# A transformer layer on one core: where residual rows are scaled, how the last pair's sum is formed, and which queue asks for the first x tile

## The chip, the core and the metric

The kernel runs on one core of a Trainium2 chip. Five engines of the core take part, each with an instruction stream of its own: TensorE (PE; its weight loads are listed as PEld), VectorE (DVE), ScalarE (ACT), GpSimd (POOL) and SyncE (SP). SP does no arithmetic here; it issues transfers, and so do ACT and POOL at some places. An engine works its stream in order: an instruction that waits holds up everything behind it on that engine, and this goes for the transfers in the queues of SP, ACT and POOL too. The 16 DMA engines of the core carry what all queues ask for.

The metric is the device time of one execution in microseconds (us). Times are compared as the median of several executions.

## The reference, cut to what matters

One layer of a streaming encoder over 1024 prompt rows and 8 x 16 = 128 sample rows of width 1024, all in float32:

```python
def trunk_layer(x, ckv_past, kpe_past, conv_past, ...):
    mix, ckv, kpe, v = token_mixer(x, ...)          # latent attention and a spatial-gating branch, then w_o
    h = layer_norm(DEEPNORM_ALPHA * x + mix, ln1_g, ln1_b)
    ff, conv_state = conv_ffn(h, conv_past, w_up, w_conv, b_conv, w_down)
    y = layer_norm(DEEPNORM_ALPHA * h + ff, ln2_g, ln2_b)
    return y, ckv, kpe, v, conv_state

def conv_ffn(x, conv_past, w_up, w_conv, b_conv, w_down):
    up = x @ w_up                                    # 1024 -> 2 * 2816
    padded = concat([conv_past, up])
    conv = b_conv + sum(w_conv[k] * padded[k:k + s_len] for k in range(3))
    a, g = split(conv, 2)
    return (silu(a) * g) @ w_down, padded[-2:]       # 2816 -> 1024
```

For this change the two uses of `h` matter: it is the input of the up projection, and `ALPHA * h` is added again at the end. `h` is a normalised row times `ln1_g` plus `ln1_b`.

## The kernel before, in words

The rows stand in nine tiles of 128 (eight of the prompt, `t` = 0 to 7, and one of samples, `t` = 8 = `NP`). Every float32 product is formed of three matmuls: an operand is split into a rounded part, which ACT copies (L60), and the rest, which DVE subtracts (L61); products are high by high, high by rest, rest by high (L72 to L74, `dmm` from L1211, `product_mm` at L936 to L938).

The stages, with their places in the profiled execution:

- **Latents (from 0).** `w1` (eight pieces `w1[k]` of 128x704) and the tiles of x, transposed (`xT`), are loaded by SP, split, and multiplied. The sample tile comes first (`ORD[0]`), in three pieces of 1, 3 and 4 blocks of 128 columns, and the pieces of `w1` are asked for in between (L183 to L197). ACT's first instruction is the load of a table.
- **Attention, gating branch, output projection, first layer norm (up to about 472 us).** At its end a tile of normalised rows, without `ln1_g` and `ln1_b`, is in `yt`, goes to the scratch tensor `nd[t]` in device memory (L843), and is transposed on PE; there ACT applies `ln1_g` and `ln1_b` for the up projection (L859).
- **Up stage (about 472 to 960 us).** 22 turns `i` of some 22.4 us. A turn has 14 products (seven combinations `STEPS` of sub-blocks for each of two halves of the rows, in the manner of Strassen), whose results ACT copies or DVE adds into the buffers `U` (L1035, L1037). POOL prepares `U` for the next turn (`new_U`, L1014 and L1015). The conv, the silu and the gate of turn `i` (`after(i)`) are a list of small functions `pend`, of which one is called behind each product of turn `i + 1`; the last of them send the results out by POOL (`ad`, `an`, `ax`). `lg1`, the row `ln1_g` spread over the partitions, is loaded at the start of the stage and lies in the last part of `cbox`.
- **Down stage (about 960 to 1218 us).** Five phases "2", "1", "65", "73", "4", each with 11 entries `p`. `produce` makes the next entry's operands: SP loads a weight tile (`raw` or `rw`) and an activation tile (`ra`), DVE forms sums of them ("65": L1133, L1134, L1146; "73": L1140), and ACT and DVE split them into slots of a ring of 14. `fill_ring` calls `produce` until the ring is full, and then the entry's matmuls are issued. The ring and two kinds of raw buffers (three and two) set how far ahead the loads may run.
- **Residual.** `first_y(t)` (L1206) loads `nd[t]` into `y[t]` and multiplies and adds on DVE (L1208, L1209, 128x1024 each). It is called at the entries 1, 3, 5, 7 of "2" and 1, 3, 5, 7, 9 of "1". `lb1`, `ln1_b` spread over the partitions, is loaded at the start of the stage (L1194). `lg2` and `lb2` are loaded at entry 2 of "1" (L1265, L1266).
- **Takes.** At the end of a phase DVE adds the PSUM banks to `y` (`take`, L1222). A bank that the next phase goes on adding to can't be written by PE until its take is done. At the end of "1" these are four takes of `X` and two of the sample tile; at the end of "65" four of `X` and four of `Z`.
- **Second layer norm and the end.** The sample tile is complete after "1". Its norm is done alone (`norm_a`, `norm_b`) at the entries 3 and 5 of "65"; SP sends it out (`out_y_s`, L1253). The even column halves of the last four tiles get their last product, phase "4", at the very end. For the last tile it is done in two quarters of 256 columns, both in the bank `X[3]`; DVE adds `ALPHA * y` and the bank (L1338), takes statistics (L1339) and normalises (L1340 to L1347).

`pin` keeps an instruction at its place in the program order; what isn't pinned may be moved by the scheduler.

Of the kernel before, what the change touches and what calls it, by code (L numbers as in the profile page):

```python
# [16 lines left out]
P = 128  # L17
D = 1024
# [24 lines left out]
def trunk(tc, a, o):  # L43
# [137 lines left out]

    ORD = [NP] + list(range(NP))
    load_w1(0)  # L183
    for t, cuts in ((ORD[0], (0, 1, 4, 8)), (ORD[1], (0, 4, 8))):
        raw = w1p.tile([P, KD, P], F32, tag="xr", name="xr", bufs=2)
        xq[t] = w1p.tile([P, 2, KD, P], F32R, tag="xs", name="xs", bufs=3)
        for k0, k1 in zip(cuts, cuts[1:]):
            ks = slice(k0, k1)
            sp.dma_start(raw[:, ks], a["xT"][t][:, ks])
            if k1 == 1:  # L190
                dve.tensor_copy(xq[t][:, 0, ks], raw[:, ks])
                dve.tensor_tensor(xq[t][:, 1, ks], raw[:, ks], f(xq[t][:, 0, ks]), ALU.subtract)
            else:
                split(xq[t][:, 0, ks], xq[t][:, 1, ks], raw[:, ks])
                load_w1(len(w1))
# [615 lines left out]
    nd = [drp.tile([P, D], F32, tag=f"nd{t}", name=f"nd{t}") for t in range(TT)]  # L811
    HT, NPF = SEQ // 2, NF // 2
    ad = [drp.tile([P, UW - 2], F32, tag=f"ad{i}", name=f"ad{i}") for i in range(NF)]
    an = [drp.tile([P, SEQ], F32, tag=f"an{i}", name=f"an{i}") for i in range(NPF)]
# [172 lines left out]
    for s in (3, 4):  # L987
        build_h(bop2, 1, s)

    cwst = raw_w()  # L990
    cw = cwst[:, :8 * NF].rearrange("p (f k) -> p f k", k=4)
# [159 lines left out]
    for i in range(NF):  # L1151
# [28 lines left out]
        while pend:  # L1180
            pend.pop(0)()
        pend = after(i)
    while pend:
        pend.pop(0)()
    pool.dma_start(o["cs"], cs)
    upool.release()
    stp.release()
# [4 lines left out]
    half = [slice(0, HT), slice(HT, D)]  # L1192
    lb1 = raw_w()
    pin(sp.dma_start(lb1, a["ln1_b"].partition_broadcast(P)))  # L1194
    y = [y2.tile([P, D], F32, tag=f"y{t}", name=f"y{t}") for t in range(4)]
# [10 lines left out]
    def first_y(t):  # L1206
        pin(sp.dma_start(y[t], nd[t]))
        pin(dve.tensor_tensor(y[t], y[t], lg1, ALU.mult))  # L1208
        pin(dve.tensor_tensor(y[t], y[t], lb1, ALU.add))  # L1209

# [49 lines left out]
    for k, (ph, p) in enumerate(ENTRY[:4 * NPF]):  # L1260
        fill_ring(2)
        if (ph, p) in ylate:
            first_y(ylate[ph, p])
        if (ph, p) == ("1", 2):
            pin(sp.dma_start(lg2, a["ln2_g"].partition_broadcast(P)))  # L1265
            pin(sp.dma_start(lb2, a["ln2_b"].partition_broadcast(P)))  # L1266
        if (ph, p) == ("65", 3):
            lone_n = norm_a([NP], [ctile[2][:, :D]])
        if (ph, p) == ("65", 5):
            norm_b(lone_n)  # L1270
# [40 lines left out]
    fin = made[4 * NPF:]  # L1311
    def end_mm(tp, cols):
        for p, (wd, ac, _) in enumerate(fin):
            dmm(X[tp][:, cols], ac, seg[tp], wd, cols, False, False, p == P1)

# [3 lines left out]
    mv = y2.tile([P, 2], F32, tag="mv", name="mv")  # L1319
    quart = [slice(e * 256, (e + 1) * 256) for e in range(4)]  # L1320
    zs = [ctile[2][:, :D]] + [new_a[1]() for _ in range(3)]
    evens = norm_a(range(4), zs)
# [4 lines left out]
    for tp in range(NT - 1):  # L1327
        take(tp + NT, 0, X[tp], True, True)
        cur = norm_a([tp + NT], [zs[tp]])
        if tp < 2:  # L1330
            end_mm(tp + 1, half[0])
        else:
            end_mm(tp + 1, quart[0])
            end_mm(tp + 1, quart[1])
        norm_b(cur)
    for e in (0, 1):
        yv = yt[:, quart[e]]
        pin(dve.scalar_tensor_tensor(yv, yv, ALPHA, X[3][:, quart[e]], ALU.mult, ALU.add))  # L1338
        pin(dve.bn_stats(s6[:, e], yv))  # L1339
# [123 lines left out]
```

## Time and profile before

| | |
|---|---|
| time, median of 3 executions | 1228.17 us (1227.75 to 1228.61) |
| the profiled execution | 1228.54 us |
| its span | 1226.8 us |
| granted TensorE clock, mean | 0.994 |
| busy: PE / DVE / ACT / POOL | 1202.2 / 917.2 / 573.0 / 100.5 us |
| bytes moved | 156.86 MB, mean 128 GB/s |

The span runs from the first to the last instruction of the profiled execution, which took 1.7 us longer than its span. PE is busy for 98% of it, so what any other engine does matters only where PE waits for it. The rows in the prediction are of these kinds. A row of the **timeline** has the start, the duration, the engine, the line and the operation, and in brackets how long the engine stood idle before it and what it waited for. A row of the **waits** has who waited for what: the sum, how often, and the longest. A row of the **windows** has a stretch of time, its length, then the busy time of PE, PEld, DVE, ACT and POOL with the number of instructions, the granted clock (1.00 is full speed), the share of the DMA engines and GB/s.

### The profile page before, as it was taken

To read this page: it belongs to the slowest core of one execution; us is meant where nothing else is said; L and a number is where in the kernel's file an instruction comes from. 1 tells how busy PE (TensorE), PEld (TensorE's weight loads), DVE (VectorE), ACT (ScalarE), POOL (GpSimd) and SP (SyncE) were. 2 spreads that over 40 slices of the span, in tenths; PEclk is the share of its full clock that TensorE was granted. 3 is DMA by queue.
4 is the path that set the end of the run, shared out by engine and by line. 5 is a ranking of instruction groups with operands and counts; after the bars stand their busy time and mean duration, and the time that the engine had idled before them with its cause. 6 is when DMAs were issued, how large, how long until landed. Compare 5 with 4: busy or idle time off the path is not lost.

```text
span 1226.8 us, 19873 instructions
## 1 busy us (share of the span) xinstructions
PE 1202.2 (98%) x7620; PEld 1117.1 (91%) x7620; DVE 917.2 (75%) x1727; ACT 573.0 (47%) x1154; POOL 100.5 (8%) x255
## 2 busy tenths in 40 slices
PE   8999999999999999999999999999999999899997
PEld 7999999989888888999999999999999988687886
DVE  5767878665557677897777778778778789987667
ACT  5434666542134546654544544545445455344431
POOL 0110002300000001121011011011011100010000
PEclk9999999999999999999999999999999999899999
DMA  7201003551023430132132133123224399878623
GB/s 255 84 21 41 33 22 95 180 176 52 1 85 133 150 120 35 58 128 100 53 116 103 50 117 117 52 100 117 72 81 163 112 401 362 320 287 315 191 78 137
DMA packets 56479, 156.86 MB, mean 128 GB/s; under 512 B 7568, under 2 KB 11536, under 8 KB 56384
## 3 DMA queue, kind: packets, MB, share of 16 engines
q1 hardware_dynamic: 47456, 124.03, 29.1%
q0 software_dynamic: 8928, 31.56, 6.8%
q8 instruction: 60, 0.98, 0.3%
q14 instruction: 35, 0.29, 0.1%
HBM read 119.29 MB, written 36.27 MB: 127 GB/s over the span
## 4 chain that ended last, share of the span: by engine, by line
PE 84%; DVE 6%; DMA 5%; ACT 2%; issue 2%; SPq 1%; DVEq 0%; ACTq 0%
PE A L938 8%; PE A L937 8%; PE A L936 8%; PE A L72 5%; PE A L73 5%; PE A L74 5%; PE D L72 4%; PE D L73 4%; PE D L74 4%; PE D L938 4%; PE D L937 4%; PE D L936 4%; DVE b L61 2%; PE B L938 2%; PE B L936 2%; PE B L937 2%
## 5 line engine op out<-in xcount | busy, mean ns | idle before, releaser
L936 PE MATMUL A<-b,wu 128*128 128x288 f32 x704 | 207.6, 296 | 0.5 <-DVE U L1035 0.4
L937 PE MATMUL A<-b,wu 128*128 128x288 f32 x704 | 207.9, 296 | 0.0
L938 PE MATMUL A<-b,wu 128*128 128x288 f32 x704 | 206.2, 298 | 0.0
L936 PEld LDWEIGHTS A<-b,wu 128*128 128x128 f32 x704 | 132.4, 188 | 1.0 <-DVE U L1035 0.6
L937 PEld LDWEIGHTS A<-b,wu 128*128 128x128 f32 x704 | 132.8, 189 | 0.0
L938 PEld LDWEIGHTS A<-b,wu 128*128 128x128 f32 x704 | 131.1, 188 | 0.0
L60 ACT ACTIVATE wu<-sc 128x512 fp32r<-128x512 f32 x66 | 41.8, 633 | 138.0 <-PE A L938 107.4
L938 PE MATMUL D<-b,wu 128*128 128x288 f32 x352 | 104.9, 298 | 0.0
L936 PE MATMUL D<-b,wu 128*128 128x288 f32 x352 | 104.1, 296 | 0.0
L937 PE MATMUL D<-b,wu 128*128 128x288 f32 x352 | 104.0, 295 | 0.0
L60 ACT ACTIVATE b<-ra 128x512 fp32r<-128x512 f32 (+1 forms) x69 | 45.3, 677 | 64.2 <-PE B L1213 18.1
L1043 DVE SCALAR_TENSOR_TENSOR cbox<-U,raw,cbox 128x1168 f32<-128x1168 f32 x44 | 62.9, 1430 | 9.3 <-ACT cbox L1042 9.3
L61 DVE TENSOR_TENSOR wu<-sc,wu 128x512 fp32r<-128x512 f32 x66 | 46.1, 699 | 29.9 <-ACT wu L60 28.4
L61 DVE TENSOR_TENSOR b<-ra,b 128x512 fp32r<-128x512 f32 (+1 forms) x69 | 50.4, 751 | 22.1 <-ACT b L60 16.0
L937 PEld LDWEIGHTS D<-b,wu 128*128 128x128 f32 x352 | 66.4, 189 | 0.0
L936 PEld LDWEIGHTS D<-b,wu 128*128 128x128 f32 x352 | 66.1, 188 | 0.3 <-ACT b L60 0.3
L938 PEld LDWEIGHTS D<-b,wu 128*128 128x128 f32 x352 | 66.1, 188 | 0.0
L1042 ACT ACTIVATE cbox<-U,raw 128x1168 f32<-128x1168 f32 x44 | 60.0, 1364 | 9.9 <-issue 5.2
L60 ACT ACTIVATE wu<-raw 128x512 fp32r<-128x512 f32 x66 | 41.6, 632 | 47.8 <-PE D L938 23.6
L1044 DVE SCALAR_TENSOR_TENSOR cbox<-U,raw,cbox 128x1168 f32<-128x1168 f32 x44 | 62.9, 1430 | 0.8
L1037 ACT ACTIVATE U<-A 128x288 f32<-128x288 f32 (+2 forms) x154 | 53.3, 369 | 20.7 <-PE A L938 20.7
L61 DVE TENSOR_TENSOR wu<-raw,wu 128x512 fp32r<-128x512 f32 x66 | 45.0, 684 | 15.9 <-ACT wu L60 15.8
(447 smaller groups left out, 3460.0 us busy)
## 6 DMA issues: line engine op xcount, KB each, us to landing
raw<-in_w_up SPq DMA_DIRECT2D x44, 512.0 KB, 3.2
raw<-in_w_down SPq DMA_DIRECT2D x28, 512.0 KB, 6.0
ad<-cbox POOLq DMA_DIRECT2D x22, 584.0 KB, 3.1
ra<-ad SPq DMA_DIRECT2D x40, 256.0 KB, 4.5
rw<-in_w_down SPq DMA_DIRECT2D x16, 512.0 KB, 5.9
xr<-in_xT SPq DMA_DIRECT2D x14, 512.0 KB, 4.0
an<-cbox POOLq DMA_DIRECT2D x11, 512.0 KB, 3.9
ra<-an SPq DMA_DIRECT2D x11, 512.0 KB, 6.8
```

What stands on the lines that cost most here:

```text
L60: act.activation(hi, src, AF.Copy)
L61: dve.tensor_tensor(lo, src, f(hi), ALU.subtract)
L72: pe.matmul(out, lh, rh, start=first, stop=False)
L73: pe.matmul(out, lh, rl, start=False, stop=False)
L74: pe.matmul(out, ll, rh, start=False, stop=last)
L936: hold(pe.matmul(o_, lh, rh, start=first and k == 0, stop=False, skip_group_check=not first))
L937: hold(pe.matmul(o_, lh, rl, start=False, stop=False, skip_group_check=not first))
L938: hold(pe.matmul(o_, ll, rh, start=False, stop=k == 3, skip_group_check=not first))
L1037: act.activation(dst, src, AF.Copy)
L1042: act.activation(v, U[:, 2:n + 2], AF.Identity, bias=cw[:, fi, 3:4], scale=cw[:, fi, 2:3])
L1043: dve.scalar_tensor_tensor(v, U[:, 1:n + 1], cw[:, fi, 1:2], v, ALU.mult, ALU.add)
L1044: dve.scalar_tensor_tensor(v, U[:, 0:n], cw[:, fi, 0:1], v, ALU.mult, ALU.add)
```

## The change

Three things are changed.

**The first x tile.** The three pieces of `xT[ORD[0]]` are asked for by ACT, ahead of its table load, and no longer by SP between the pieces of `w1`.

**The residual rows.** `ln1_g` and `ln1_b` are applied in the up stage. `scale_rows(j)`, for `j` = 0 to 17, does one half (512 columns) of one tile: POOL loads the piece of `nd[t]`, DVE multiplies and adds, POOL stores the piece to a new scratch tensor `hd[t]`. The halves of `ln1_b` are loaded by POOL, twice 128x512. One call stands at the third place of `pend` in each of the turns 1 to 18. `first_y` only loads `hd[t]`, and the load of `lb1` is gone. With that, three things of the down stage move: the loads of `lg2` and `lb2` from entry 2 of "1" to entry 1 of "73", and the two parts of the sample tile's norm from the entries 3 and 5 of "65" to 4 and 6 of "73".

**The end.** The two quarters of the last tile's last product go to two banks of their own (`XL`), and `ALPHA * y` plus the bank `X[3]` is formed ahead of it. The adds behind the product are plain ones of 256 columns.

```diff
@@ latents
     ORD = [NP] + list(range(NP))
+    xraw = [w1p.tile([P, KD, P], F32, tag="xr", name="xr", bufs=2) for _ in range(2)]
+    for k0, k1 in ((0, 1), (1, 4), (4, 8)):
+        tc.keep_in_program_order(act.dma_start(xraw[0][:, k0:k1], a["xT"][ORD[0]][:, k0:k1]))
     load_w1(0)
     for t, cuts in ((ORD[0], (0, 1, 4, 8)), (ORD[1], (0, 4, 8))):
-        raw = w1p.tile([P, KD, P], F32, tag="xr", name="xr", bufs=2)
+        raw = xraw[0] if t == ORD[0] else xraw[1]
...
-            sp.dma_start(raw[:, ks], a["xT"][t][:, ks])
+            if t == ORD[1]:
+                sp.dma_start(raw[:, ks], a["xT"][t][:, ks])
@@ up stage
+    hd = [drp.tile([P, D], F32, tag=f"hd{t}", name=f"hd{t}") for t in range(TT)]
...
+    hx = alloc("hx", side="right")
+
+    def scale_rows(j):
+        c, t = divmod(j, TT)
+        cols = slice(c * 512, (c + 1) * 512)
+        lb = hx.tile([P, 512], F32, tag="lb", name="lb") if t == 0 else lbs[0]
+        if t == 0:
+            lbs[:] = [lb]
+            pool.dma_start(lb, a["ln1_b"][cols].partition_broadcast(P))
+        v = hx.tile([P, 512], F32, tag="hv", name="hv")
+        pool.dma_start(v, nd[t][:, cols])
+        dve.tensor_tensor(v, v, lg1[:, cols], ALU.mult)
+        dve.tensor_tensor(v, v, lb, ALU.add)
+        pool.dma_start(hd[t][:, cols], v)
+
+    lbs = []
...
         pend = after(i)
+        if 1 <= i <= 2 * TT:
+            pend.insert(2, lambda i=i: scale_rows(i - 1))
...
+    hx.release()
@@ down stage
-    lb1 = raw_w()
-    pin(sp.dma_start(lb1, a["ln1_b"].partition_broadcast(P)))
...
     def first_y(t):
-        pin(sp.dma_start(y[t], nd[t]))
-        pin(dve.tensor_tensor(y[t], y[t], lg1, ALU.mult))
-        pin(dve.tensor_tensor(y[t], y[t], lb1, ALU.add))
+        pin(sp.dma_start(y[t], hd[t]))
...
-        if (ph, p) == ("1", 2):
+        if (ph, p) == ("73", 1):
             pin(sp.dma_start(lg2, a["ln2_g"].partition_broadcast(P)))
             pin(sp.dma_start(lb2, a["ln2_b"].partition_broadcast(P)))
-        if (ph, p) == ("65", 3):
+        if (ph, p) == ("73", 4):
             lone_n = norm_a([NP], [ctile[2][:, :D]])
-        if (ph, p) == ("65", 5):
+        if (ph, p) == ("73", 6):
             norm_b(lone_n)
@@ end
-    def end_mm(tp, cols):
+    def end_mm(tp, cols, out=None):
         for p, (wd, ac, _) in enumerate(fin):
-            dmm(X[tp][:, cols], ac, seg[tp], wd, cols, False, False, p == P1)
+            if out is None:
+                dmm(X[tp], ac, seg[tp], wd, cols, False, False, p == P1)
+            else:
+                dmm(out, ac, seg[tp], wd, cols, True, p == 0, p == P1)
...
+    XL = [bank("D") for _ in range(2)]
+    pin(dve.scalar_tensor_tensor(yt[:, half[0]], yt[:, half[0]], ALPHA, X[3], ALU.mult, ALU.add))
...
-            end_mm(tp + 1, quart[0])
-            end_mm(tp + 1, quart[1])
+            for e in range(2):
+                end_mm(tp + 1, quart[e], XL[e][:, :256])
...
-        pin(dve.scalar_tensor_tensor(yv, yv, ALPHA, X[3][:, quart[e]], ALU.mult, ALU.add))
+        pin(dve.tensor_tensor(yv, yv, XL[e][:, :256], ALU.add))
```

At the end of phase "1", DVE's stream before was this; the numbered `y0` to `y3` and `cbox` ahead of the arrow in the rows of L1222 are the residual tiles that the six takes add to, `A`, `B`, `C` the PSUM banks, and the rows of L1133, L1134 and L1146 form the operands of entry 4 of "65":

```order
L1208 TENSOR_TENSOR cbox_5515<-cbox_5515 128x1024
L61 TENSOR_TENSOR b17_5498<-ra_11493,b17_5498 128x1024
L1133 TENSOR_TENSOR rw_11529<-rw_11529 128x512
L1209 TENSOR_TENSOR cbox_5515<-cbox_5515,raw_10843 128x1024
L1134 TENSOR_TENSOR rw_11529<-raw_11531,rw_11529 128x512
L1146 TENSOR_TENSOR raw_11531<-raw_11531,rw_11529 128x512
L1222 SCALAR_TENSOR_TENSOR y0_10845,sums_10855<-y0_10845,A_11216 128x512
```

The same place of the same stream with the change, where the lines are numbered 20 or 21 higher:

```order
L61 TENSOR_TENSOR b17_5507<-ra_11580,b17_5507 128x1024
L1154 TENSOR_TENSOR rw_11614<-rw_11614 128x512
L1155 TENSOR_TENSOR rw_11614<-raw_11616,rw_11614 128x512
L1167 TENSOR_TENSOR raw_11616<-raw_11616,rw_11614 128x512
L1242 SCALAR_TENSOR_TENSOR y0_10950,sums_10960<-y0_10950,A_11313 128x512
```

The multiply and the add of the last residual tile (L1208, L1209) are gone from between the operands; the takes stand where they stood, behind the three sums of entry 4 of "65".

At the end of phase "65", SP's stream before had the store of the sample tile, `out_y_s`, between the loads of the last entry of "65" (L1131, L1132) and those of the first entry of "73" (L1136 to L1139):

```order
L1131 DMA raw_11772<-in_w_down 128x1024
L1132 DMA ra_11769<-an10_4485 128x1024
L1253 DMA out_y_s<-cbox_5515 128x1024
L1136 DMA raw_11816<-in_w_down 128x512
L1137 DMA raw_11816<-in_w_down 128x512
```

With the change SP's stream has it far behind, between the loads of the entries 1 and 2 of "4":

```order
L1141 DMA ra_12295<-ad3_4465 128x512
L1142 DMA raw_12296<-td1_4507 128x512
L1273 DMA out_y_s<-cbox_5527 128x1024
L1141 DMA ra_12335<-ad5_4467 128x512
L1142 DMA rw_12336<-td2_4508 128x512
```

The store, and with it the wait for the norm of the sample tile, has moved behind all loads of "73".

At the head, SP's stream before went back and forth between pieces of `w1` (L152) and pieces of the first x tile (`xr_107`, L189):

```order
L152 DMA raw_102<-in_w1 128x704
L189 DMA xr_107<-in_xT 128x128
L189 DMA xr_107<-in_xT 128x384
L152 DMA raw_115<-in_w1 128x704
L189 DMA xr_107<-in_xT 128x512
L152 DMA raw_123<-in_w1 128x704
```

With the change ACT's stream begins with these three pieces (L185), and its splits of `w1[0]` and `w1[1]` (L60) both come ahead of that of the second x piece:

```order
L185 DMA xr_102<-in_xT 128x128
L185 DMA xr_102<-in_xT 128x384
L185 DMA xr_102<-in_xT 128x512
L60 ACT_TABLE_LOAD
L60 ACTIVATE w1_0_109<-raw_107 128x704
L60 ACTIVATE w1_1_119<-raw_117 128x704
L60 ACTIVATE xs_112<-xr_102 128x384
```

SP is left with the pieces of `w1` alone, one behind the other, up to the third.

## The prediction

> **What bounds the kernel now.** First the page, to see which engine sets the end, then the waits of that engine.
>
> ```profile
> span 1226.8 us, 19873 instructions
> ...
> PE 84%; DVE 6%; DMA 5%; ACT 2%; issue 2%; SPq 1%; DVEq 0%; ACTq 0%
> ```
>
> The chain that ended last runs 84% over PE. So time is won only where PE stands idle, where it runs at a lower clock, and behind its last product. Its waits are few:
>
> ```profile
> PE A L72 <- ACT w L60: 5.8, 2, 4.7
> PE A L1212 <- DVE y L1222: 4.8, 2, 2.9
> ...
> PE D L1214 <- DVE b L61: 1.1, 1, 1.1
> ...
> PE A L936 <- DVE U L1035: 0.4, 1, 0.4
> ```
>
> The first row is the head, the second and third are the ends of the phases "1" and "65". The last is all that the up stage's 22 turns make PE wait for DVE's adds into U. Then the windows, which show what a pause costs beside itself, and how full the other engines are:
>
> ```profile
> 545.00:580.00 35.00, 35.00 (x265) 35.00 (x264) 27.11 (x40) 15.44 (x32) 3.94 (x12) 1.00 0.27 97
> 1000.00:1040.00 40.00, 40.00 (x179) 33.11 (x178) 38.35 (x53) 21.99 (x36) 0.00 (x0) 1.00 1.00 365
> 1066.68:1072.84 6.16, 6.16 (x15) 4.83 (x16) 6.16 (x14) 1.34 (x2) 0.29 (x1) 0.54 0.46 161
> 1125.95:1130.60 4.65, 4.65 (x13) 3.66 (x14) 4.65 (x9) 1.21 (x2) 0.00 (x0) 0.63 0.91 346
> 1140.00:1160.00 20.00, 20.00 (x90) 16.57 (x89) 11.57 (x13) 9.90 (x13) 0.00 (x0) 1.00 0.52 162
> ```
>
> In the up stage (first row) PE is full and DVE busy for 27.11 of 35 us. In the down stage (second row) DVE and the DMA engines are both full: 38.35 of 40, and a share of 1.00. There PE runs on a stock of operands that DVE and the loads can only just fill. The next two rows are what follows the two pauses: clock 0.54 and 0.63. At full clock a matmul of these phases takes 40.00 / 179 = 0.223 us (second row). So 15 matmuls should take 3.35 us and took 6.16, 2.81 lost; 13 should take 2.90 and took 4.65, 1.75 lost.
>
> **Residual rows, first place: the end of "1".**
>
> ```profile
> 1063.01 0.73 PE L1214 MATMUL D<-b,b 128*128 128x512 f32 x2 [1.10 <-DVE b L61]
> 1066.68 0.80 PE L1212 MATMUL A<-b,b 128*128 128x512 f32 x1 [2.94 <-DVE y L1222]
> ...
> 1060.60 1.22 DVE L1208 TENSOR_TENSOR cbox<-cbox 128x1024 f32<-128x1024 f32 x1
> 1061.74 1.22 DVE L61 TENSOR_TENSOR b<-ra,b 128x1024 fp32r<-128x1024 f32 x1
> 1063.47 1.22 DVE L1209 TENSOR_TENSOR cbox<-cbox,raw 128x1024 f32<-128x1024 f32 x1
> 1064.61 0.68 DVE L1134 TENSOR_TENSOR rw<-raw,rw 128x512 f32<-128x512 f32 x1
> 1065.94 0.68 DVE L1222 SCALAR_TENSOR_TENSOR y<-y,A 128x512 f32<-128x512 f32 x1
> ...
> 1064.96 1.06 ACT L60 ACTIVATE b<-ra 128x1024 fp32r<-128x1024 f32 x1 [4.59 <-DMA ra<-an]
> ```
>
> PE pauses 1.10 for a split that stood behind L1208, and 2.94 for the first take, which stood behind L1209 and the sums of the next entry. With the lost clock this place costs 1.10 + 2.94 + 2.81 = 6.85 us. The change takes away 9 multiplies and 9 adds of 1.22, so 22 us of DVE's work between 992 and 1065:
>
> ```profile
> L1208 DVE TENSOR_TENSOR y<-y,cbox x7: 1218/1218/1219, 992.3 to 1049.2; 128x1024 f32<-128x1024 f32 x7
> ...
> L908 DVE TENSOR_TENSOR sc<-raw 128x512 f32<-128x512 f32 x17 | 11.6, 684 | 1.5 <-DMA raw<-in_w_up 1.4
> 558.78 0.52 DVE L1035 TENSOR_TENSOR U<-U,A 128x160 f32<-128x160 f32 x2 [1.68 <-PE A L938]
> 565.03 0.10 POOL L1014 MEMSET U<- 128x2 f32 x1 [3.83 <-ACT U L1037]
> td<-raw POOLq DMA_DIRECT2D x3, 256.0 KB, 4.8
> ```
>
> It also takes 1.5 MB of loads out of this stretch (lb1, lg2 and lb2, 0.5 MB each, the last two moved behind it), which at the 365 GB/s of the second window are 4.1 us of full DMA engines. What is late next is the sum of entry 4 of "65", which the takes still stand behind. Its weights had landed by 1064.61 at the latest, where L1134 reads them; its activations (ACT's row, landed near 1064.9) aren't in the sum. Even if that was their landing, with the loads 4.1 earlier L1134 could run at 1060.5, and two sums and a take of 0.69 each let PE go on near 1062.6. Without the pause of 1.10 PE runs out of other work at 1066.68 - 2.94 - 1.10 = 1062.6. So by the loads alone, at their worst, the pause is about nil; by DVE, with 22 us less, it is nil with room. I take the whole 6.85 as gone, with 0.3 left over for a take that is just late. If the loads gain nothing, since they only run further ahead, the 2.94 and its clock stay: a rival below.
>
> **Second place: the end of "65".**
>
> ```profile
> SPq L1131 <- DVE b L61: 31.3, 8, 6.7
> SPq L1253 <- DVE cbox L1252: 11.2, 1, 11.2
> ...
> 1109.57 0.69 DVE L1140 TENSOR_TENSOR raw<-raw 128x512 f32<-128x512 f32 x1 [5.38 <-DMA raw<-in_w_down]
> 1123.99 1.21 DVE L61 TENSOR_TENSOR b<-ra,b 128x1024 fp32r<-128x1024 f32 x1
> 1125.13 0.67 DVE L1222 SCALAR_TENSOR_TENSOR y<-y,A 128x512 f32<-128x512 f32 x1
> 1125.95 0.47 PE L1212 MATMUL A<-b,b 128*128 128x512 f32 x1 [1.92 <-DVE y L1222]
> ```
>
> SP waits 11.2 us with the store of the sample tile at the head of its queue; behind it are all loads of "73". DVE therefore idles 5.38 us, then makes up leeway, and comes to the takes 1.92 us late. With the lost clock: 1.92 + 1.75 = 3.7 us. The store is moved behind those loads, so they are asked for up to 11 us earlier, DVE has its 5.38 back, and the takes come in time. What the moved parts bring to "73" (1 MB for lg2 and lb2, two DVE passes of the norm) meets slack: in 1140 to 1160 (last window) DVE is busy for 11.57 of 20 us and the DMA share is 0.52. The store itself now waits for L1272 ahead of loads for the entries 2 and on of "4", which are several entries of 24 x 0.223 = 5.4 us away from use. Costed at nothing; without that cover it would be a pause like this one, 3.7. First row: SP's 31.3 us of waits on DVE's splits also shrink.
>
> **The price in the up stage.** 18 pieces, each with two DVE operations of 128x512 at 0.684 (L908's row), 1.37 us a turn. DVE has (35.00 - 27.11) / 35 of a turn of 22.4 us idle, 5.0; a single wait of DVE for PE is 1.68 (row at 558.78). PE waited for DVE 0.4 us in the whole stage. So I cost it at nothing. On POOL a piece adds a load, a store and their waits in order: the next load waits for the store's landing (`hv` has one buffer), and the preparation of U is behind it. A transfer of 256 KB from POOL took 4.8 us to land where the DMA engines were full, so load, two operations and store take some 11 us of a turn; POOL idled 3.83 us ahead of a single memset. Bounds: nothing, or all of it on the path, 18 x 1.37 = 24.7. Nearest is nothing, because DVE's idle time in a turn is over three times the price.
>
> **The end.**
>
> ```profile
> 1213.56 1.28 DVE L1252 SCALAR_TENSOR_TENSOR y<-ra,ry,cbox 128x1024 f32<-128x1024 f32 x1
> 1218.09 0.42 DVE L1338 SCALAR_TENSOR_TENSOR cbox<-cbox,B 128x256 f32<-128x256 f32 x1 [3.24 <-PE B L1214]
> 1218.55 0.43 DVE L1339 BATCH_NORM_STATS2 s<-cbox 128x6 f32<-128x256 f32 x1
> 1218.89 0.40 DVE L1338 SCALAR_TENSOR_TENSOR cbox<-cbox,B 128x256 f32<-128x256 f32 x1
> ...
> 1222.96 0.75 DVE L1347 SCALAR_TENSOR_TENSOR cbox<-cbox,ry 128x512 f32<-128x512 f32 x1
> ```
>
> Both quarters wait for PE's last matmul, since they are in one bank, though the first quarter's product was complete 33 matmuls earlier. In banks of their own the first add and its statistics run inside the 3.24 us in which DVE stood idle, and the second add starts at 1218.09 where it started at 1218.89: 0.80 won. The new 128x512 operation (0.68, as L1222) stands earlier, among the takes; DVE's 3.24 idle us hide it.
>
> **The head.**
>
> ```profile
> 3.86 0.79 ACT L60 ACTIVATE w<-raw 128x704 fp32r<-128x704 f32 x1 [1.84 <-DMA raw<-in_w]
> 5.19 0.52 ACT L60 ACTIVATE xs<-xr 128x384 fp32r<-128x384 f32 x1 [0.54 <-DMA xr<-in_xT]
> 7.39 0.79 ACT L60 ACTIVATE w<-raw 128x704 fp32r<-128x704 f32 x1 [1.68 <-DMA raw<-in_w]
> 8.23 0.69 PE L72 MATMUL A<-w,xs 128*128 128x384 f32 x1 [1.06 <-ACT w L60]
> ```
>
> PE's second start, at 8.23, waits for the second weight piece. It needs the same bytes in both versions; SP now issues that piece right behind the first. At best the wait of 1.06 goes. At worst the second x piece lands together with the weights, and its split, 0.52, follows the weights' on ACT, as the new order has it: +0.5. The table load ends ahead of the first split either way (ACT idled 1.84). I take 0. [...] No row here shows two queues sharing at the head.
>
> **The sum.** 1228.54 - 6.85 - 3.67 - 0.80 + 0 + 0.3 = 1217.5. The profiled execution lies 0.37 above the median, so I predict 1217.2 us, 0.9% faster.
>
> **The rivals.**
> - One pause stays. The takes at the end of "1" still stand behind loads; if the DMA engines stay full and entry 4 lands as late as before, only the 1.10 of that place is won: 1217.2 + 2.94 + 2.81 = 1222.9. If instead the "65" takes, now behind sums of two entries of "73", are late again: 1217.2 + 3.7 = 1220.9. For it: DMA share 1.00; against: 1.5 MB less and 31.3 us of SP's waits on DVE.
> - Shared queues at the head. PE starts again 0.5 later: 1217.7. As said, only the order of ACT's splits speaks for it.
> - Nothing but the end is won: the loads, not DVE, set both places. 1228.2 - 0.8 = 1227.4. Against it stands DVE's queue in the two timelines.
> - Slower: in the up stage the pieces hold DVE's adds into U or, by POOL, the preparation of U, and PE waits in every turn. It decides from 11.0 / 18 = 0.6 us a turn; with the whole 1.37 it is 1217.2 + 24.7 = 1241.9. For it: POOL works strictly in order and a piece has two landings; against it the idle time above.
>
> Should a pause be left over, its price is open. After 1.92 us of pause the clock was 0.63 over 4.65 us, so I count a pause nearly double. [...]
>
> **How the numbers follow.** Both pauses gone, the head anywhere between -1.06 and +0.5: 0.63 (of it 0.2 for the shared queues). One pause stays: 0.19. Nothing: 0.07. Slower: 0.11. A measurement of this kernel tells a change of about 0.2%, 2.5 us, from none; so faster 0.82, same 0.07, slower 0.11. The range leaves out the last two cases: from 1214.8 (the head's best, and 1.4 for further waits of SP) to 1224.0.
>
> **What would show it.** Right: no wait of L1232 on a take over 0.3 us; granted clock 1.00 in the stretches after the ends of "1" and "65"; SP's wait with `out_y_s` no longer ahead of L1157; the first quarter's add ahead of PE's end. PE full in the up stage's windows, with DVE 1.4 us a turn busier. Wrong: waits of L936 to L938 on U that recur every turn; the first take behind a row "<-DMA ra<-an"; a second start of PE later than 8.7.

## The result, and the profile after

| | before | after |
|---|---|---|
| median of 4 executions | 1227.96 us | 1215.47 us (1214.77 to 1217.03) |
| profiled execution / its span | 1228.54 / 1226.8 us | 1215.77 / 1213.9 us |
| mean granted clock | 0.994 | 0.998 |

The ratio is 0.9901, with a 95% interval of 0.9889 to 0.9914: 12.5 us less. The prediction was 1217.2 us, with a range from 1214.8 to 1224.0.

The page of the changed kernel, engines and chain:

```profile
span 1213.9 us, 19977 instructions
...
PE 1195.6 (98%) x7620; PEld 1113.9 (92%) x7620; DVE 918.9 (76%) x1746; ACT 574.5 (47%) x1154; POOL 126.0 (10%) x293
...
PE 94%; ACT 2%; DMA 2%; DVE 1%; issue 0%; SPq 0%; ACTq 0%
```

PE's share of the chain went from 84% to 94%, DVE's from 6% to 1%, and that of the transfers from 5% to 2%. PE has 6.6 us less busy time for the same 7620 matmuls, mostly from stretches at half clock that are gone (0.50 for 6.83 and 3.41 us in before). Its waits:

```profile
PE A L72 <- ACT w L60: 5.1, 1, 5.1
...
PE D L72 <- ACT wuv L60: 0.6, 1, 0.6
...
PE B L1232 <- ACT b L60: 0.4, 1, 0.4
PE A L941 <- DVE U L1056: 0.4, 1, 0.4
```

No row names a take (L1242) or a split of DVE. The wait on U in the up stage is 0.4 us as before. At the head one wait is left of two. The wait of 0.6 is new; it is at 264 us, where ACT splits a weight 1.1 us earlier than before (263.61 against 264.71) while PE comes 2.3 us earlier. The trace of e5 below, the same kernel once more, doesn't have it.

The timeline at the end of "1", DVE and PE:

```profile
1057.65 0.69 DVE L1167 TENSOR_TENSOR raw<-raw,rw 128x512 f32<-128x512 f32 x1
1058.26 0.68 DVE L1242 SCALAR_TENSOR_TENSOR y<-y,A 128x512 f32<-128x512 f32 x1
...
1060.32 0.61 PE L1234 MATMUL D<-b,b 128*128 128x512 f32 x2
1060.78 0.39 PE L1232 MATMUL A<-b,b 128*128 128x512 f32 x1
```

The first take starts 7.7 us earlier than before, and PE goes from the products into D to those into A without a pause. At the end of "65":

```profile
1113.54 0.68 DVE L1242 SCALAR_TENSOR_TENSOR y<-y,A 128x512 f32<-128x512 f32 x1
...
1114.95 0.39 PE L1234 MATMUL A<-b,b 128*128 128x512 f32 x1
1115.18 0.39 PE L1232 MATMUL A<-b,b 128*128 128x512 f32 x1
```

The take is done 0.96 us ahead of the matmul that needs it. Three windows of the down stage:

```profile
1000.00:1040.00 40.00, 40.00 (x178) 33.11 (x177) 29.96 (x45) 22.32 (x36) 0.55 (x1) 1.00 0.97 367
...
1060.00:1075.00 15.00, 15.00 (x68) 12.43 (x67) 14.40 (x23) 4.23 (x5) 1.20 (x3) 1.00 0.83 308
...
1112.00:1125.00 13.00, 13.00 (x59) 10.77 (x58) 13.00 (x18) 4.42 (x5) 0.00 (x0) 1.00 0.98 370
```

DVE is busy for 29.96 us of the first one, where it was 38.35; PE is full and at full clock in all three. The end:

```profile
1202.40 0.42 DVE L1363 TENSOR_TENSOR cbox<-cbox,D 128x256 f32<-128x256 f32 x1
1202.85 0.43 DVE L1364 BATCH_NORM_STATS2 s<-cbox 128x6 f32<-128x256 f32 x1
1205.57 0.42 DVE L1363 TENSOR_TENSOR cbox<-cbox,D 128x256 f32<-128x256 f32 x1 [2.29 <-PE D L1234]
```

The first quarter's add and statistics are over before PE's last matmul. And the head:

```profile
5.58 0.79 ACT L60 ACTIVATE w<-raw 128x704 fp32r<-128x704 f32 x1 [0.57 <-DMA raw<-in_w]
...
5.06 0.69 PE L72 MATMUL A<-w,xs 128*128 128x384 f32 x1 [5.06 <-ACT w L60]
7.33 0.52 PE L72 MATMUL A<-w,xs 128*128 128x384 f32 x1
```

The second weight piece is split from 5.58 on, where it was 7.39. PE starts 0.36 later and then doesn't pause.

Both traces have the same 7620 matmuls, so the start of the n-th one can be compared, and the lead shows where the time was won:

| n, place | before | after | lead |
|---|---|---|---|
| 301, in the latents | 55.86 | 53.52 | 2.34 |
| 1691, behind the new wait | 265.92 | 264.51 | 1.41 |
| 6665, in "2" | 997.14 | 995.72 | 1.42 |
| 6965, in "65" | 1072.38 | 1063.72 | 8.66 |
| 7191, last of "65" | 1123.65 | 1114.95 | 8.70 |
| 7204, in "73" | 1130.34 | 1117.90 | 12.44 |
| 7620, the last | 1217.77 | 1205.25 | 12.52 |

So the end of "1" gave 8.66 - 1.42 = 7.2 us, the end of "65" 12.44 - 8.70 = 3.7, the head 2.3, of which 1.4 were left at 1000 us (2.6 and 2.0 in the trace of e5). From the start of PE's last matmul to the end of the span it is 9.00 us before and 8.68 after, 0.3 less.

### The profile page after: what moved, and what is told of

The parts are those of the page before. It is cut to its first block, busy times and chain, and to the rows that moved or that the text cites. A ratio compares the mean times of both kernels' runs of the same rounds, so it can differ in the third digit from the quotient of the medians.

```text
span 1213.9 us, 19977 instructions
## 1 busy us (share of the span) xinstructions
PE 1195.6 (98%) x7620; PEld 1113.9 (92%) x7620; DVE 918.9 (76%) x1746; ACT 574.5 (47%) x1154; POOL 126.0 (10%) x293
## 4 chain that ended last, share of the span: by engine, by line
PE 94%; ACT 2%; DMA 2%; DVE 1%; issue 0%; SPq 0%; ACTq 0%
PE A L943 8%; PE A L942 8%; PE A L941 8%; PE A L72 4%; PE D L72 4%; PE A L73 4%; PE A L74 4%; PE D L73 4%; PE D L74 4%; PE D L943 4%; PE D L942 4%; PE D L941 4%; PE A L1233 2%; PE A L1232 2%; PE A L1234 2%; PE B L943 2%
## 5 line engine op out<-in xcount | busy, mean ns | idle before, releaser
L60 ACT ACTIVATE wu<-sc 128x512 fp32r<-128x512 f32 x66 | 41.8, 633 | 137.7 <-PE A L943 114.2
L60 ACT ACTIVATE b<-ra 128x512 fp32r<-128x512 f32 (+1 forms) x69 | 45.2, 677 | 52.6 <-DMA ra<-ad 25.7
L61 DVE TENSOR_TENSOR b<-ra,b 128x512 fp32r<-128x512 f32 (+1 forms) x69 | 50.4, 752 | 23.9 <-ACT b L60 20.9
L60 ACT ACTIVATE wu<-raw 128x512 fp32r<-128x512 f32 x66 | 41.6, 631 | 43.9 <-PE D L943 23.3
```

The costliest lines, as they stand in the source:

```text
L60: act.activation(hi, src, AF.Copy)
L61: dve.tensor_tensor(lo, src, f(hi), ALU.subtract)
```

## The experiments

Each kernel is the changed one with the edit that is shown. Each was timed beside the kernel before on the same chip; the interval of a ratio is about 0.13% wide on each side, 1.6 us. Smaller differences are read from the traces. e9 to e11 ran on a chip on which the kernel before took 1229.31 us, where it took 1227.8 to 1228.4 beside the others, so their medians are compared with one another, or by the ratio.

| run | median us | ratio to before (95%) |
|---|---|---|
| e1, old head | 1217.02 | 0.9911 (0.9898 to 0.9923) |
| e2, old end | 1215.50 | 0.9897 (0.9882 to 0.9911) |
| e3, old places of loads and norm | 1221.66 | 0.9945 (0.9929 to 0.9962) |
| e4, rows scaled in the down stage | 1218.21 | 0.9922 (0.9910 to 0.9934) |
| e5, the changed kernel again | 1214.72 | 0.9894 (0.9879 to 0.9909) |
| e6, old place of lg2 and lb2 alone | 1215.62 | 0.9902 (0.9888 to 0.9915) |
| e7, as e3 | 1221.13 | 0.9953 (0.9940 to 0.9965) |
| e8, three times the operations in the pieces | 1215.35 | 0.9899 (0.9886 to 0.9913) |
| e9, one queue in another order | 1216.90 | 0.9899 (0.9884 to 0.9914) |
| e10, one piece by ACT | 1215.74 | 0.9892 (0.9878 to 0.9907) |
| e11, first weight piece in two | 1218.43 | 0.9913 (0.9896 to 0.9929) |
| e12, as e3, store by POOL | 1214.81 | 0.9894 (0.9878 to 0.9911) |

### The end of "1": operations or loads?

e4 puts the multiplies and adds, and lb1, back into the down stage:

```diff
+    lb1 = raw_w()
+    pin(sp.dma_start(lb1, a["ln1_b"].partition_broadcast(P)))
...
-        pin(sp.dma_start(y[t], hd[t]))
+        pin(sp.dma_start(y[t], nd[t]))
+        pin(dve.tensor_tensor(y[t], y[t], lg1, ALU.mult))
+        pin(dve.tensor_tensor(y[t], y[t], lb1, ALU.add))
...
-        if 1 <= i <= 2 * TT:
-            pend.insert(2, lambda i=i: scale_rows(i - 1))
```

> The changed kernel with the residual rows scaled in the down stage again (18 operations of 1.22 us on DVE, lb1 loaded there), everything else as changed, so lg2 and lb2 are still loaded behind the end of 1. Theory of the prediction, DVE's queue makes the first pause: the pauses of 1.1 and 2.9 us at the end of 1 and the half clock are back, +6.9 us, 1222.4; the end of 65 stays without a pause. Rival, the loads make it: with only 0.5 MB more loads in that stretch the pause is 1 us or less, +0 to +2, 1215.5 to 1217.5. If the pieces cost anything in the up stage, that is won here: PE's time from the first to the last product of the up stage would be shorter by it.

Measured: 1218.21 us, and in the trace one pause. DVE and PE there:

```profile
1059.30 1.22 DVE L1213 TENSOR_TENSOR cbox<-cbox,raw 128x1024 f32<-128x1024 f32 x1
1060.43 0.69 DVE L1138 TENSOR_TENSOR rw<-raw,rw 128x512 f32<-128x512 f32 x1
1061.16 0.69 DVE L1150 TENSOR_TENSOR raw<-raw,rw 128x512 f32<-128x512 f32 x1
1061.76 0.68 DVE L1226 SCALAR_TENSOR_TENSOR y<-y,A 128x512 f32<-128x512 f32 x1
...
1062.51 0.50 PE L1216 MATMUL A<-b,b 128*128 128x512 f32 x1 [1.81 <-DVE y L1226]
```

DVE works without a gap up to the take, and an add of the residual (L1213) stands 2.5 us ahead of it. The pause is 1.81 us; with the lowered clock behind it (0.69 from 1062.5 to 1068.0) PE falls back by 3.7 us here against the changed kernel, about half of 7.2. So the moved loads alone (lg2 and lb2, 1 MB, are still behind this place in e4) win about half, and neither theory was right as it stood. The load of lb1 and the buffer that it holds come back together with the operations, but they aren't what makes this pause: lb1 is asked for at 965.7 us and lands 3.5 us later, and from 1000 us up to the take DVE never waits for a landing. It is busy for 61.70 of 62 us, where it is 49.49 in the changed kernel:

```profile
1000.00:1062.00 62.00, 60.70 (x268) 49.92 (x266) 61.70 (x80) 31.09 (x44) 2.19 (x4) 1.00 0.97 359
```

e6 puts only these two loads back:

```diff
-        if (ph, p) == ("73", 1):
+        if (ph, p) == ("1", 2):
             pin(sp.dma_start(lg2, a["ln2_g"].partition_broadcast(P)))
             pin(sp.dma_start(lb2, a["ln2_b"].partition_broadcast(P)))
```

> The changed kernel with only the loads of lg2 and lb2 (1 MB) back at entry 2 of 1; rows scaled in the up stage, norm of the sample tile late. With the rows scaled below and these loads moved, the end of 1 had still one pause of 1.8 us and cost 3.5 us of the 7.2 that it cost before. Theory, operations and loads add up: a pause of the same order by the loads alone, +2 to +3.7 us, 1217.5 to 1219.2. Rival, without the 18 operations there is room for the loads: no pause, 1215.5.

Measured: 1215.62 us, no pause, and the first take within 0.12 us of its time in the changed kernel:

```profile
1058.14 0.68 DVE L1242 SCALAR_TENSOR_TENSOR y<-y,A 128x512 f32<-128x512 f32 x1
```

The rival holds. The two parts don't add up: without the 18 operations there is room for the loads, and then moving the loads is worth nothing; with the operations in place, moving the loads is worth half. Taking out the operations suffices for the whole 7.2.

### The end of "65"

e3 has the old places of both, the loads and the norm:

```diff
-        if (ph, p) == ("73", 1):
+        if (ph, p) == ("1", 2):
...
-        if (ph, p) == ("73", 4):
+        if (ph, p) == ("65", 3):
             lone_n = norm_a([NP], [ctile[2][:, :D]])
-        if (ph, p) == ("73", 6):
+        if (ph, p) == ("65", 5):
             norm_b(lone_n)
```

> The changed kernel with the loads of lg2 and lb2 and the norm of the sample tile at their old places, entries 2 of 1, 3 and 5 of 65. Theory of the prediction: SP waits with out_y_s ahead of all loads of 73 again, so the pause at the end of 65 is back, +3.7 us, 1219.2, while the end of 1 stays without a pause, since DVE is relieved. Rival 1, relief of DVE is enough at both places: 1215.5, no pause. Rival 2, the loads decide the end of 1: with 1 MB more of them there the pause of some 3 us and its half clock is back, +5 to +7 on top: 1224 to 1226.

Measured: 1221.66 us, but the profiled execution of these took only 1216.4. So the same kernel was run once more.

> The kernel of e3 once more: loads of lg2 and lb2 and the norm of the sample tile at the old places. Its profiled execution took 1216.4 us with one pause of 1.8 us at the end of 65 and no lowered clock behind it, the other five 1221.2 to 1224.2. Theory: the clock is lowered or not by chance behind such a pause; then a profile of a long execution shows the same pause and one stretch of 3.4 us at half clock, which is only 1.7 us, 1218; the rest up to 1222 must be a second pause, at the end of 1. Rival: the profile of a long execution shows a longer pause at the end of 65 alone.

Measured: 1221.13 us, and this time the profiled execution was a long one, 1222.99. Both have one pause, and it is at the end of "65". SP, DVE and PE of e3:

```profile
1093.80 0.34 SPq L1273 DMA_DIRECT2D out_y_s<-cbox  x1
...
1114.98 0.68 DVE L1242 SCALAR_TENSOR_TENSOR y<-y,A 128x512 f32<-128x512 f32 x1
...
1115.81 0.47 PE L1232 MATMUL A<-b,b 128*128 128x512 f32 x1 [1.76 <-DVE y L1242]
```

The same of e7, with the norm's last operation (L1272) and DVE's first sum of "73" (L1161):

```profile
1098.51 0.34 SPq L1273 DMA_DIRECT2D out_y_s<-cbox  x1
...
1097.20 1.29 DVE L1272 SCALAR_TENSOR_TENSOR cbox<-cbox,ry 128x1024 f32<-128x1024 f32 x1
1103.41 0.69 DVE L1161 TENSOR_TENSOR raw<-raw 128x512 f32<-128x512 f32 x1 [4.92 <-DMA raw<-in_w_down]
1119.52 0.68 DVE L1242 SCALAR_TENSOR_TENSOR y<-y,A 128x512 f32<-128x512 f32 x1
...
1120.34 0.77 PE L1232 MATMUL A<-b,b 128*128 128x512 f32 x1 [6.51 <-DVE y L1242]
```

From the row of the store to the first take it is 1114.98 - 1093.80 = 21.2 us in e3, 21.0 in e7, and 1125.13 - 1104.21 = 20.9 in the kernel before: five entries (five rows of L1161 in each of the traces of e3 and e7) are loaded and built in that time, and it is nearly the same in all three, though PE is earlier or later. The pause is what is left when PE is earlier than that. Before, PE came to this place late, since it had paused at the end of "1", and lost 1.92 us here; with that first pause gone and the store at its old place it loses 1.76 or 6.51. The rival of e7's expectation holds: one place, a longer pause. With the clock at 1.00 behind 1.76 us (e3, 1115.81 to 1118.60) and at 0.53 behind 6.51 (e7, 1120.34 to 1125.00) this makes the two times: against the changed kernel PE falls back here by 2.0 us in e3 and by 8.8 in e7.

e12 keeps the old places and lets POOL ask for that one store:

```diff
-            sp.dma_start(o["y_p"][t * P:(t + 1) * P] if t < NP else o["y_s"], y[t])
+            if t < NP:
+                sp.dma_start(o["y_p"][t * P:(t + 1) * P], y[t])
+            else:
+                pool.dma_start(o["y_s"], y[t])
```

> The kernel of e3 and e7 (loads of lg2 and lb2 and the sample tile's norm at the old places), with one more edit: the store of the sample tile is asked for by POOL, whose queue has nothing behind it, and not by SP. Theory, SP's queue makes the pause at the end of 65: no pause there, 1215 to 1216 us, and the 20.9 us that lay between that store's issue and the first take in all three profiles with it no longer bind. Rival, the norm's own work on DVE at that place (two operations of 1.28 us and small ones) makes it: the pause stays, 1221 us.

Measured: 1214.81 us, and no wait of PE on a take. DVE and POOL:

```profile
1095.05 0.69 DVE L1161 TENSOR_TENSOR raw<-raw 128x512 f32<-128x512 f32 x1
...
1095.84 1.29 DVE L1272 SCALAR_TENSOR_TENSOR cbox<-cbox,ry 128x1024 f32<-128x1024 f32 x1
...
1097.53 0.54 POOL L1276 DMA_DIRECT2D out_y_s<-cbox  x1 [4.67 <-DVE cbox L1272]
...
1110.93 0.68 DVE L1242 SCALAR_TENSOR_TENSOR y<-y,A 128x512 f32<-128x512 f32 x1
```

DVE forms the first sum of "73" (L1161) before the norm's last operation is even done, and the take comes 13.4 us behind the store. The norm costs DVE the same as in e7. So it was SP's queue that made the pause, and taking one store out of it does what the move of the norm and of the loads does.

### The pieces in the up stage

e8 adds four operations to each piece:

```diff
         dve.tensor_tensor(v, v, lb, ALU.add)
+        for _ in range(4):
+            dve.tensor_tensor(v, v, v, ALU.max)
```

> The changed kernel with four more operations of 128x512 on DVE in each piece (each takes the maximum of the piece with itself, which changes nothing), so 18 x 4 x 0.6 to 0.68 us = 43 to 49 us more in the up stage, six times 0.68 = 4.1 us a turn where the prediction counted 5.0 us of idle time. Theory of the prediction: hidden, 1215.5 to 1216.5. Rival: the idle time lies where DVE must wait for PE and can't take it up; every turn then loses up to 2.7 us, up to 1264.

Measured: 1215.35 us. The up stage in windows of equal length, first of before, then of after, then of e8:

```profile
501.50:947.50 446.00, 446.00 (x3345) 446.00 (x3344) 353.80 (x525) 218.93 (x405) 57.48 (x163) 1.00 0.27 96
```

```profile
500.00:946.00 446.00, 446.00 (x3343) 446.00 (x3342) 373.46 (x561) 219.53 (x404) 81.68 (x199) 1.00 0.33 117
```

```profile
500.00:946.00 446.00, 446.00 (x3344) 446.00 (x3343) 410.19 (x632) 219.82 (x405) 127.43 (x199) 1.00 0.32 116
```

DVE's busy time rises by 20 and by another 37 us, and PE is full in all three. The rows of the two operations show that the pieces weren't one a turn:

```profile
L1006 DVE TENSOR_TENSOR hv<-hv,cbox x18: 678/684/696, 500.5 to 687.8; 128x512 f32<-128x512 f32 x18
```

18 of them from 500.5 to 687.8 us are one each 11 us, two a turn: the scheduler drew them ahead, and they still cost nothing.

### The end

e2 has both quarters in `X[3]` again:

```diff
-            for e in range(2):
-                end_mm(tp + 1, quart[e], XL[e][:, :256])
+            end_mm(tp + 1, quart[0])
+            end_mm(tp + 1, quart[1])
...
-        pin(dve.tensor_tensor(yv, yv, XL[e][:, :256], ALU.add))
+        pin(dve.scalar_tensor_tensor(yv, yv, ALPHA, X[3][:, quart[e]], ALU.mult, ALU.add))
```

> The changed kernel with both quarters of the last product in the bank X[3] again. By the prediction +0.8 us, 1216.3: the second quarter's add starts 1.1 us behind PE's last matmul and not 0.3. Rival: from the two spans only 0.35 us was won behind PE's last matmul (9.03 to 8.68 us), so +0.35.

Measured: 1215.50 us, which at this size says nothing. In the trace the two adds stand as before the change:

```profile
1205.78 0.42 DVE L1358 SCALAR_TENSOR_TENSOR cbox<-cbox,B 128x256 f32<-128x256 f32 x1 [3.24 <-PE B L1234]
...
1206.58 0.41 DVE L1358 SCALAR_TENSOR_TENSOR cbox<-cbox,B 128x256 f32<-128x256 f32 x1
```

From the start of PE's last matmul (1205.47 here) to the second add it is 1.11 us, in the changed kernel 0.32, before 1.12; to the end of the span 9.46, 8.68 and 9.00. Against e2 the new end is worth the 0.8 of the prediction. That before is 0.5 better than e2 lies mostly behind the last landing: 1.03 us from there to the end of the span in before, 1.45 in e2 and in after. This is 1.38 to 1.45 in eleven of the twelve traces with pieces in the up stage (1.15 in e12), and 1.02 in the other one without, e4. Its cause wasn't tried.

### The head

e1 lets SP ask for all pieces in the old order:

```diff
-    xraw = [w1p.tile([P, KD, P], F32, tag="xr", name="xr", bufs=2) for _ in range(2)]
-    for k0, k1 in ((0, 1), (1, 4), (4, 8)):
-        tc.keep_in_program_order(act.dma_start(xraw[0][:, k0:k1], a["xT"][ORD[0]][:, k0:k1]))
...
-            if t == ORD[1]:
-                sp.dma_start(raw[:, ks], a["xT"][t][:, ks])
+            sp.dma_start(raw[:, ks], a["xT"][t][:, ks])
```

> The changed kernel with only the first x tile asked for by SP again, between the pieces of w1. By the prediction (the head is worth nothing, -1.06 to +0.5) it stays at 1215.5 us, and PE's second start is no later. By the trace of after (PE is 2.4 us ahead of before at 57 us, and 1.5 us ahead from 265 us on) it is 1217.0 us, with the second start again at 8.2 us and the wait of 0.57 us for a weight split at 264 us gone. If the rest of that lead has another cause, it is nearer 1215.5.

Measured: 1217.02 us, 1.5 over the changed kernel's first median and 2.3 over its second (e5). The second start is back:

```profile
8.16 0.69 PE L72 MATMUL A<-w,xs 128*128 128x384 f32 x1 [1.03 <-ACT w L60]
```

and the time is that of the second reading of the expectation. The new wait at 264 us is gone too, but the changed kernel's second trace (e5) doesn't have it either, so it says nothing of the head. By e1's trace PE is 1.2 us behind the changed kernel at the 301st matmul, 0.3 behind the new wait, and 0.9 at the last. Before the change it was 2.3 at the 301st with the same head; the difference is the clock, which rose to full speed at 14.2 us in that trace, at 11.7 in e1's and at 10.7 in the changed kernel's. The rows of the matmuls show it: one of 128x384 takes 0.52 us ahead of that time and 0.34 behind it, and the next starts 0.32 and 0.18 us later. (The clock in the rows of the windows below is 1.00 although PE isn't at full clock yet.) By these spacings some 45% of the time by which the clock rises later is lost: about 1.6 of the 2.3 us between before and after, and 0.5 of the 1.2 between e1 and after. What the traces of before and after show of its rise is in the last section.

e9 keeps one queue, with the second weight piece ahead of the second x piece; in e10 ACT asks for the first x piece alone (the edit shown is that of e10):

```diff
-    for k0, k1 in ((0, 1), (1, 4), (4, 8)):
+    for k0, k1 in ((0, 1),):
...
+            if t == ORD[0] and k0 > 0:
+                load_w1(len(w1))
-            if t == ORD[1]:
+            if t == ORD[1] or k0 > 0:
                 sp.dma_start(raw[:, ks], a["xT"][t][:, ks])
```

> The changed kernel with all of the head's loads on SP's queue again, but in another order: the second weight piece third instead of fourth, ahead of the second x piece. Theory A, the order of what is needed: half of the gain or more stays, the second weight piece lands near 6.5 us (7.4 before, 5.6 with ACT's queue) and PE's second start is at 7.5 us. Theory B, one queue can't keep the DMA engines full and it takes a second one: the piece lands 0.5 us earlier at best, by the 192 KB that no longer go ahead of it at 400 GB/s, so the second start is at 7.7 to 8.2 us and the time 0.5 to 1 us over the changed kernel's.

> The changed kernel with only the first x piece (64 KB) asked for by ACT, the second and third by SP behind the second and third weight piece. Theory A, what counts is that SP's second weight piece is asked for 0.9 us earlier: PE's second start stays at 7.3 us, and the first start comes back to 4.7 us, since less goes beside the first weight piece. Theory B, two queues must be at work: the second weight piece lands over 6 us, second start over 7.5 us.

Measured: 1216.90 and 1215.74 us. PE's second start of e9, then the first and second of e10:

```profile
8.31 0.69 PE L72 MATMUL A<-w,xs 128*128 128x384 f32 x1 [1.19 <-ACT xs L60]
```

```profile
5.01 0.69 PE L72 MATMUL A<-w,xs 128*128 128x384 f32 x1 [5.01 <-ACT w L60]
...
7.28 0.52 PE L72 MATMUL A<-w,xs 128*128 128x384 f32 x1
```

In e9 the weight piece landed at 6.7, as theory A had it, but now the second x piece was late (7.7), and the start is later than in e1. With 64 KB of all these bytes on a second queue the start is at 7.28. So another order in one queue gained nothing here (8.31 in e9, 8.16 in e1): the second start needs both the second weight piece and the second x piece, and the one that came second was the late one, the x piece in e9 (split from 7.74) and the weight piece in e1 (7.32). From 4 to 6 us the DMA engines moved, in the windows of before, e9, e10 and after:

```profile
4.00:6.00 2.00, 1.30 (x3) 0.88 (x4) 1.66 (x4) 1.17 (x2) 0.00 (x0) 1.00 0.79 203
```

```profile
4.00:6.00 2.00, 1.35 (x3) 0.92 (x4) 1.41 (x3) 0.60 (x1) 0.00 (x0) 1.00 0.76 223
```

```profile
4.00:6.00 2.00, 0.99 (x3) 0.56 (x3) 1.45 (x4) 1.58 (x2) 0.00 (x0) 1.00 0.95 291
```

```profile
4.00:6.00 2.00, 0.94 (x3) 0.51 (x3) 1.41 (x3) 1.21 (x2) 0.00 (x0) 1.00 1.02 375
```

203 and 223 GB/s with one queue, 291 and 375 with two. The first start doesn't come back in e10 (5.01, where the changed kernel has 5.06), so it isn't delayed by how much follows on the second queue. In this point theory A of e10 was wrong.

e11 is e10 with the first weight piece loaded and split in two:

```diff
-        sp.dma_start(raw, a["w1"][k])
...
-        split(w[:, 0], w[:, 1], raw)
+        for cs_ in (slice(0, RQ), slice(RQ, NW1)) if k == 0 else (slice(0, NW1),):
+            sp.dma_start(raw[:, cs_], a["w1"][k][:, cs_])
+            split(w[:, 0, cs_], w[:, 1, cs_], raw[:, cs_])
```

> As e10, and the first weight piece is loaded and split in two parts of 384 and 320 columns, so that the first product can start on half of it. If the first start bounds the head now: first start 0.4 to 0.8 us earlier than in e10, and PE that much earlier at 60 us; about 0.5 us less than the changed kernel, too little for the medians. If the later pieces bound it, PE pauses behind the first products and is no earlier at 60 us.

Measured: 1218.43 us. First and second start:

```profile
4.06 0.69 PE L72 MATMUL A<-w,xs 128*128 128x384 f32 x1 [4.06 <-ACT w L60]
...
7.71 0.69 PE L72 MATMUL A<-w,xs 128*128 128x384 f32 x1 [1.43 <-ACT xs L60]
```

PE starts 0.95 us earlier, pauses 1.43, and is 2.3 us later at the 301st matmul (56.10 against 53.75 in e10), some 1.5 of it by the clock, which rose at 13.7 us and not at 10.4. An early start that isn't followed up is worth less than none.

The run shows more: ACT asks for the first x piece as in e10, so two queues are at work, but from 4 to 6 us the DMA engines move hardly more than with one:

```profile
4.00:6.00 2.00, 1.94 (x6) 1.71 (x6) 1.09 (x3) 0.40 (x2) 0.00 (x0) 1.00 0.84 226
```

So the second queue alone didn't fill them here (a share of 0.84). The second weight piece is now third in SP's queue, as in e9. In these runs its landing goes with the time at which SP asks for it: asked for at 1.2 us its split starts at 5.13 (e10) and 5.58 (the changed kernel), at 1.65 us at 6.46 (e11) and 6.72 (e9), at 2.12 us at 7.32 (e1) and 7.39 (before). Why asking 0.46 us later makes it land 0.7 to 1.6 us later isn't shown.

### The changed kernel again

> The changed kernel itself once more, beside the others on one chip. All theories: 1215.5 us, no pause at the ends of 1 and 65. What it tells is how far executions of one kernel lie apart: where the clock is lowered behind the pause of 1.1 us at 249 us and up to when it is low at the head.

Measured: 1214.72 us, no pause at either end. No kernel here is better than the changed one by more than its interval.

## Why the prediction was right, point by point

- **The end of "1"**: predicted 6.85, measured 7.2. Mechanism shown by e4 and e6: taking DVE's operations out suffices. The statement that the loads alone would nearly do it ("by the loads alone, at their worst, the pause is about nil") was wrong: with the loads moved and the operations left (e4), 1.81 us of pause stay, and DVE is full. It counted 1.5 MB out of this stretch; lb1 was asked for at 967.1 us, ahead of it, so it was 1 MB, 2.7 us at the same 365 GB/s and not 4.1.
- **The end of "65"**: predicted 3.67, measured 3.7; the cause, SP's queue, is shown by e12. What was wrong is the price if this part were missing: the rival "one pause stays" counted 3.7 for it, and e3 and e7 are 6 us over the changed kernel. The prediction treated the two places as terms that add up; but this pause ends some 21 us behind the store's issue, so much of what is won at the first place can be lost here again (8.8 us lost here in e7 against 3.7 before, but 2.0 in e3, where the store went out earlier).
- **The up stage**: predicted nothing, measured nothing, with room for three times the operations (e8). That it is one piece a turn was wrong, it is two; so the price was carried by the idle time even at twice the rate that the prediction counted.
- **The end**: predicted 0.80 and shown by e2 against the changed kernel; 0.4 of it is given back behind the last landing, in a way that isn't settled.
- **The head**: the mis-sized term. Taken as 0, it was worth 2.3 us at 56 us between the two traces and 1.4 at 1000 us; against e1, where less of it is the clock, 1.2 and 0.9, and 1.5 to 2.3 in the medians. The step that failed is "It needs the same bytes in both versions": that made the start a question of bytes, where the DMA engines weren't full (0.79 from 4 to 6 us in the window of before) and the second weight piece landed earlier by more than SP asked for it earlier. What the sum had no term for at all is the clock, which behind PE's second pause rose 3.5 us later in before than in after; that is the larger part of the 2.3. The better bound, -1.06, was nearer, but it is the length of the pause alone, so that it is near is partly luck. The rival "Shared queues at the head" fell: PE's second start came 0.9 us earlier (7.33 against 8.23) and not 0.5 later. In e10 SP asks for the second weight piece 0.46 us earlier than in e9, and PE starts again 1.03 earlier; but in e11, also with two queues, SP asks for it as late as in e9, and its split starts 1.33 us later than in e10. So the time saved in asking was worth more than itself, and that the second queue does more than save it isn't shown.
- **The sum**: 1217.2 against 1215.5. The head's 1.4 and the 0.3 for a late take that didn't come make the 1.7 between them; the end of "1" gave 0.4 more and the end 0.5 less than counted, and that these cancel is luck.

## What to carry to other kernels

In the kernel before, a store in the queue that also loads held all loads behind it for the 11.2 us until its producer was done, with the DMA engines at a share of 0.45 (1093.0 to 1104.2). Look for such a store first where an engine idles for a landing though the DMA engines have been free, and give it to a queue with nothing behind it, as in e12. When two pauses follow each other, ask whether the second ends at a time that the first doesn't move: removing the first alone can then just lengthen it (1.92 us before, 6.51 in e7). Work that stood in the way at a tight place cost nothing in a stage where the bounding engine was full (446.00 of 446.00 us, with 20 us more of DVE's work), and trebling it there (another 37 us, e8) was a cheap test of that.

## What the runs showed of the hardware that wasn't expected

The changes of the granted clock lie whole multiples of 3.413 us (92.16 / 27) apart in the trace of before, which has them at 14.21, 1065.52, 1072.34, 1126.95 and 1130.37 us and behind the last product at 1222.53: the stretches between are 1051.3 us (308 times that), 6.83 (2), 54.61 (16), 3.41 (1) and 92.16 (27). In after it changed at 10.69 and at 1208.76, 1198.08 us apart (351 times). After pauses of 1.92 us (before, end of "65") and 1.81 us (e4) a stretch of 3.41 us went at half clock, and after 1.76 us (e3) none. Of e3, where PE goes on behind that pause:

```profile
1115.81:1118.60 2.79, 2.79 (x12) 2.33 (x13) 2.79 (x6) 1.06 (x1) 0.00 (x0) 1.00 1.02 368
```

Behind the pause of 1.1 us at 249 us in before (ahead of L534), and the same pause in after (L538), the clock stayed at 1.00 too (246 to 260 and 244 to 258 us). So the price of a pause of 1 to 2 us was its length here, or some 1.7 us more, half of 3.41; what decides between the two isn't shown. This may be one reason why executions of one kernel here differ by a microsecond or two. Why the store came 4.7 us later in e7 than in e3, two executions of the same kernel, is open.

At the head the clock rose at 14.21 us in before and at 10.69 in after. Counted back from there in steps of 3.41 us, PE in before stood idle for 0.94 us of the stretch from 3.97, for 0.85 of the one from 7.38 and for none of the one from 10.80 to 14.21; in after for 1.21 of the one from 3.86 and for none of the one from 7.27 to 10.69. The stretches that end with the rises at 1072.34 and 1130.37 us in before have no idle time either; the one from 1065.52, at half clock with another behind it, has 1.16. PE's second pause at the head, of 1.0 to 1.4 us, came with more than its length: the clock rose at 14.2, 11.7 and 13.7 us in before, e1 and e11, which have it, and at 10.7 and 10.4 in after and e10, which don't. It differs between executions with the same head, as 14.2 in before and 11.7 in e1 show.
